# Column sums on one core: the framework's own semaphores, and a block's two rows added before the sum so far

## The chip, the cores and the metric

One core of a Trainium2 chip. The metric is device time in microseconds (us) for one execution. Every time below is a median over several executions; every run that lists a state was in the fast one, and the granted TensorE clock was 0.997 to 1.000 in every profile that the argument rests on, so clock plays no part.

## The reference

```python
x = np.random.randn(8192, 8192).astype(np.float32)
def reference(x):
    return np.sum(x, axis=0)
```

256 MiB have to be read once, and 32 KB are written. There is almost nothing to compute.

## The kernel before

The 8192 rows are cut into 32 blocks of 256 rows. A block is a tile of 128 partitions by K = 2 rows by 8192 columns (64 KB per partition, 8.39 MB). The kernel uses three such buffers. VectorE adds each block into a running sum with two adds of 128x8192; for the last block TensorE does the sum across partitions (a matmul with ones), in strips, so that little is left after the last byte arrives. Loads are issued by SyncE. Synchronisation is by hand, inside one critical section, with a loop on VectorE:

```python
def block(b):
    r0, r1 = bufs[b][:, 0, :], bufs[b][:, 1, :]
    take(s_buf[b], 17)            # this block has landed (16) and the sum so far is ready (1)
    nc.vector.tensor_tensor(out=r0, in0=r0, in1=bufs[(b - 1) % NBUF][:, 1, :], op=ADD
        ).then_inc(s_op, 1)       # first add: row 0 + the sum so far, from the previous buffer
    take(s_op, 1)
    nc.vector.sem_inc(s_free, 1)  # the previous buffer is free
    nc.vector.tensor_tensor(out=r1, in0=r1, in1=r0, op=ADD
        ).then_inc(s_buf[(b + 1) % NBUF], 1)   # second add: row 1 + that

# ... cut ...
for t in range(last):
    i = nc.sync.dma_start(out=bufs[t % NBUF][:], in_=xr[t])
    if t >= NBUF:
        i._wait_ge(s_free, t - NBUF + 1)       # a load waits until its buffer is free
    i.then_inc(s_buf[t % NBUF], 16)
# ... cut: the last block's strips, matmuls, copies and stores ...
```

## Time and profile before

| | before |
|---|---|
| time, median of 3 (lowest to highest) | 628.84 us (628.51 to 630.31) |
| span of the profiled run | 626.6 us |
| load queue's packets, share of 16 DMA engines' span | 99.1% |
| VectorE busy | 530.8 us, 85% |

The page of the profiled run, cut to four lines. The first `q1` line is the load queue: packets, megabytes, share of the 16 engines' span. An `L...` line is a group of instructions: line, engine, operation, shapes, count, then busy us and mean ns of one, then idle us just before them and what ended it. The last line is a group of loads with the median us from issue to landing.

```profile
span 626.6 us, 548 instructions
...
q1 hardware_dynamic: 6144, 268.47, 99.1%
...
L115 DVE TENSOR_TENSOR buf<-buf,buf 128x8192 f32<-128x8192 f32 x29 | 252.1, 8693 | 58.4 <-DVEq L110 58.4
L120 DVE TENSOR_TENSOR buf<-buf 128x8192 f32<-128x8192 f32 x29 | 252.1, 8693 | 6.9 <-DVEq L110 6.9
...
buf<-in_x_dram SPq DMA_DIRECT2D x31, 29.7
```

The reader should see three things. Loading is the limit: the queue's packets fill 99.1% of the engines' time. VectorE's two adds take 17.4 us of a block and it then waits about 2 us (58.4 us over 29 blocks), so it is close behind but not the limit. And a load lands 29.7 us after its issue although a block takes only 19.3: it stands in the queue for some 10 us before its turn.

VectorE's timeline (start us, duration us, what, idle before) shows the period. From one first add to the next are 119.85 to 139.16, 19.31 us:

```profile
119.85 8.69 DVE L115 TENSOR_TENSOR buf<-buf,buf 128x8192 f32<-128x8192 f32 x1 [1.66 <-DVEq L110]
128.78 8.69 DVE L120 TENSOR_TENSOR buf<-buf 128x8192 f32<-128x8192 f32 x1 [0.24 <-DVEq L110]
139.16 8.69 DVE L115 TENSOR_TENSOR buf<-buf,buf 128x8192 f32<-128x8192 f32 x1 [1.70 <-DVEq L110]
```

Three stretches by windows: up to the landing of block 2, from there to the landing of block 30 (28 blocks), and the rest. After the window's bounds come its length, the busy time of each engine, the clock, the DMA share and GB/s:

```profile
core 0: us, PE busy (x) PEld busy (x) DVE busy (x) ACT busy (x) POOL busy (x), PEclk, DMA share, GB/s
0.00:61.46 61.46, 0.00 (x0) 0.00 (x0) 26.08 (x3) 1.28 (x1) 0.33 (x5) 1.00 1.00 427
61.46:602.68 541.22, 0.00 (x0) 0.00 (x0) 486.79 (x56) 0.00 (x0) 0.00 (x0) 1.00 1.00 433
602.68:626.60 23.92, 13.58 (x136) 3.81 (x136) 17.91 (x6) 2.29 (x4) 0.00 (x0) 1.00 0.82 339
```

In the middle stretch the 16 engines are at 1.00 and move 433 GB/s; 541.22 / 28 = 19.33 us a block.

### The profile page before, as it was taken

The page shows a single profiled execution, that of the slowest core. Times are in us where ns is not written, and L with a number is a line of the kernel's source. Part 1 is how long each engine was busy: PE and PEld are TensorE (multiplying, and loading weights), DVE is VectorE, ACT ScalarE, POOL GpSimd, SP SyncE. Part 2 cuts the span into 40 slices and gives each one's busy share as a digit, 9 for nine tenths or more (in the row PEclk, how much of TensorE's full clock was granted, in tenths as well). Part 3 has the DMA queues.
Part 4 walks back from the last instruction along what each step waited for, and adds up shares of the span by engine and source line. Part 5 has one row for each costly group of instructions (what it writes and reads, how often), then busy time and mean ns, then how long its engine had stood idle before and what let it go on. Part 6 is the DMA issues. An engine that isn't in the chain of part 4 may idle for free. (4 is left out here: it accounts for less than half of the span.)

```text
span 626.6 us, 548 instructions
## 1 busy us (share of the span) xinstructions
PE 13.6 (2%) x136; PEld 3.8 (1%) x136; DVE 530.8 (85%) x65; ACT 3.6 (1%) x5; POOL 0.3 (0%) x5
## 2 busy tenths in 40 slices
PE   0000000000000000000000000000000000000026
PEld 0000000000000000000000000000000000000002
DVE  0538988889888899888898888988889988889886
ACT  0000000000000000000000000000000000000001
POOL 0000000000000000000000000000000000000000
PEclk9999999999999999999999999999999999999999
DMA  9999999999999999999999999999999999999987
GB/s 402 402 469 402 469 402 464 406 456 414 448 423 443 427 435 435 431 439 406 464 402 469 402 469 402 469 402 469 402 469 402 469 402 469 402 469 402 469 382 291
DMA packets 6153, 268.49 MB, mean 428 GB/s; under 512 B 636, under 2 KB 892, under 8 KB 1416
## 3 DMA queue, kind: packets, MB, share of 16 engines
q1 hardware_dynamic: 6144, 268.47, 99.1%
q8 instruction: 1, 0.02, 0.0%
q10 hardware_dynamic: 8, 0.00, 0.0%
HBM read 268.44 MB, written 0.03 MB: 428 GB/s over the span
## 5 line engine op out<-in xcount | busy, mean ns | idle before, releaser
L115 DVE TENSOR_TENSOR buf<-buf,buf 128x8192 f32<-128x8192 f32 x29 | 252.1, 8693 | 58.4 <-DVEq L110 58.4
L120 DVE TENSOR_TENSOR buf<-buf 128x8192 f32<-128x8192 f32 x29 | 252.1, 8693 | 6.9 <-DVEq L110 6.9
L126 DVE TENSOR_TENSOR buf<-buf 128x8192 f32<-128x8192 f32 x1 | 8.7, 8693 | 23.0 <-DVEq L110 23.0
L93 PE MATMUL ps<-buf,ones 128*32 128x512 f32 (+4 forms) x136 | 13.6, 549 | 609.4 <-DMA buf<-in_x_dram 609.0
L72 DVE TENSOR_TENSOR buf<-buf,buf 128x4096 f32<-128x4096 f32 x2 | 8.8, 4423 | 1.6 <-DMA buf<-in_x_dram 1.6
L72 DVE TENSOR_TENSOR buf<-buf 128x2048 f32<-128x2048 f32 (+1 forms) x3 | 8.9, 3001 | 0.1
L93 PEld LDWEIGHTS ps<-buf,ones 128*32 128x32 f32 x136 | 3.8, 118 | 619.0 <-DMA buf<-in_x_dram 611.7
L201 ACT COPY res<-ps 128x512 f32<-128x512 f32 (+1 forms) x4 | 2.3, 573 | 618.8 <-PE ps L93 618.8
L205 DVE COPY res<-ps 128x64 f32<-128x64 f32 x1 | 0.2, 225 | 2.6 <-PE ps L93 2.6
L201 ACT ACT_TABLE_LOAD x1 | 1.3, 1283 | 0.9 <-SPq L100 0.9
L101 POOL MEMSET ones<- 128x32 f32 x1 | 0.1, 124 | 0.5 <-SPq L100 0.5
L238 POOL MEMSET const-bfloat16-1.0<- 128x1 bf16 x1 | 0.1, 101 | 0.0
L238 POOL MEMSET const-uint8-127<- 128x1 uint8 x1 | 0.1, 101 | 0.0
L238 POOL MEMSET const-float32-0.0<- 128x1 f32 x1 | 0.1, 98 | 0.2 <-issue 0.2
L238 POOL MEMSET const-float32-1.0<- 128x1 f32 x1 | 0.1, 98 | 0.0
## 6 DMA issues: line engine op xcount, KB each, us to landing
buf<-in_x_dram SPq DMA_DIRECT2D x3, 2048.0 KB, 19.4
buf<-in_x_dram SPq DMA_DIRECT2D x1, 1024.0 KB, 25.5
buf<-in_x_dram SPq DMA_DIRECT2D x1, 768.0 KB, 26.8
buf<-in_x_dram SPq DMA_DIRECT2D x31, 29.7
buf<-in_x_dram SPq DMA_DIRECT2D x1, 256.0 KB, 22.6
out_dram<-res SPq DMA_DIRECT2D x1, 24.0 KB
out_dram<-res ACTq DMA_DIRECT2D x1, 1.0 KB
out_dram<-res SPq DMA_DIRECT2D x1, 7.0 KB
```

Source lines behind the costliest of these rows:

```text
L72: i = nc.vector.tensor_tensor(out=o, in0=a, in1=b, op=ADD)
L93: i = nc.tensor.matmul(out=o, lhsT=ones[:], rhs=r, start=start, stop=True, skip_group_check=True)
L101: nc.gpsimd.memset(ones[:], 1.0).then_inc(s_one, 1)
L115: nc.vector.tensor_tensor(out=r0, in0=r0, in1=bufs[(b - 1) % NBUF][:, 1, :], op=ADD).then_inc(s_op, 1)
L120: nc.vector.tensor_tensor(out=r1, in0=r1, in1=r0, op=ADD).then_inc(s_buf[(b + 1) % NBUF], 1)
L126: nc.vector.tensor_tensor(out=rows(0, 1), in0=rows(0, 1), in1=rows(0, 0), op=ADD).then_inc(s_buf[1], 1)
L201: i = nc.scalar.copy(res[:, 512 * g : 512 * g + w], ps[g][:, 0:w])
L205: i = nc.vector.tensor_copy(out=res[:, fin], in_=ps[4][:, 0:NI])
L238: nc = _bacc.Bacc("TRN2", target_bir_lowering=False, num_devices=1)
```

## The change

The intent is the same kernel without hand-made synchronisation: the framework (Tile) places the semaphores and frees the buffers, no critical section, no loop, the order of instructions on each engine kept by edges without semaphores. Along with this, the running sum moves from row 1 to row 0, and the two adds of a block change places: first the block's own two rows, then the sum so far. Strips and the order of the last matmuls change slightly, and two matmuls are added that only keep TensorE busy.

The diff, cut to its core:

```diff
-        def block(b):
-            r0, r1 = bufs[b][:, 0, :], bufs[b][:, 1, :]
-            take(s_buf[b], 17)
-            nc.vector.tensor_tensor(
-                out=r0, in0=r0, in1=bufs[(b - 1) % NBUF][:, 1, :], op=ADD
-            ).then_inc(s_op, 1)
-            take(s_op, 1)
-            nc.vector.sem_inc(s_free, 1)
-            nc.vector.tensor_tensor(out=r1, in0=r1, in1=r0, op=ADD).then_inc(
-                s_buf[(b + 1) % NBUF], 1
-            )
...
+    load_pool = ctx.enter_context(tc.tile_pool(name="loads", bufs=3))
...
+    prev = None
+    for t in range(T - 2):
+        xt = load_pool.tile([P, K, C], F32, tag="xt")
+        nc.sync.dma_start(out=xt, in_=xr[t])
+        add(xt[:, 0], xt[:, 0], xt[:, 1])
+        if prev is not None:
+            add(xt[:, 0], xt[:, 0], prev[:, 0])
+        prev = xt
+    near = load_pool.tile([P, K, C], F32, tag="xt")
+    nc.sync.dma_start(out=near, in_=xr[T - 2])
...
-STRIPS = [2048, 2048, 2048, 1024, 768, 256]
+STRIPS = [2048, 2048, 2048, 896, 896, 256]
...
+    keep_busy(last[:, 1, 0:512], 2)
```

The previous buffer is read by the add that takes in the sum so far. When that add comes first, the buffer is free after one add; when it comes second, after two.

More of the change, by code (lines that the diff above doesn't have):

```diff
@@ L12 @@
 K = 2
-NBUF = 3
+NJ = 4
 GROUP = 2048
-NJ = 4
-UNIT = 256
-NI = UNIT // NJ
-STRIPS = [2048, 2048, 2048, 1024, 768, 256]
+STRIPS = [2048, 2048, 2048, 896, 896, 256]
+START = [sum(STRIPS[:n]) for n in range(len(STRIPS))]
 @with_exitstack
@@ L32 @@
     T = R // (P * K)
-    near, last = T - 2, T - 1
     xr = x.rearrange("(b p k) c -> b p k c", p=P, k=K)
-    pool = ctx.enter_context(tc.tile_pool(name="sb", bufs=1))
+    const_pool = ctx.enter_context(tc.tile_pool(name="const", bufs=1))
+    load_pool = ctx.enter_context(tc.tile_pool(name="loads", bufs=3))
     psum_pool = ctx.enter_context(
@@ L41 @@
     )
-    ones = pool.tile([P, 32], F32, name="ones", tag="ones")
-    bufs = [
-        pool.tile([P, K, C], F32, name=f"buf{b}", tag=f"buf{b}") for b in range(NBUF)
-    ]
-    res = pool.tile([P, C // NJ], F32, name="res", tag="res")
-    ps = [
-        psum_pool.tile([P, 512], F32, name=f"ps{g}", tag=f"ps{g}") for g in range(5)
-    ]
-    s_buf = [nc.alloc_semaphore(f"s_buf{b}") for b in range(NBUF)]
-    s_strip = [nc.alloc_semaphore(f"s_strip{i}") for i in range(len(STRIPS))]
-    s_one = nc.alloc_semaphore("s_one")
@@ L56 @@
-    s_op = nc.alloc_semaphore("s_op")
-    s_free = nc.alloc_semaphore("s_free")
-    s_dve = nc.alloc_semaphore("s_dve")
-    s_pe = nc.alloc_semaphore("s_pe")
-    s_act = nc.alloc_semaphore("s_act")
-    s_end = nc.alloc_semaphore("s_end")
-    s_out = nc.alloc_semaphore("s_out")
-    def rows(t, k, c0=0, w=None):
-        return bufs[t % NBUF][:, k, c0 : C if w is None else c0 + w]
-    n_dve = 0
-    def vadd(o, a, b, sem, val):
-        nonlocal n_dve
-        i = nc.vector.tensor_tensor(out=o, in0=a, in1=b, op=ADD)
-        i._wait_ge(sem, val)
-        i.then_inc(s_dve, 1)
-        n_dve += 1
-        return n_dve
@@ L78, in column_sums @@
-    def column_sums(src, c0, w, start, sem=None, val=0):
-        g, f = divmod(c0, GROUP)
-        for j in range(NJ):
-            if g < 3:
-                assert (f, w) == (0, GROUP)
-                o = ps[g][32 * j : 32 * j + 32, :]
-                r = src[:, c0 + 512 * j : c0 + 512 * j + 512]
-            else:
-                u, n = f // UNIT, w // UNIT
-                b, q = (4, 0) if u == 7 else (3, u)
-                o = ps[b][32 * j : 32 * j + 32, NI * q : NI * (q + n)]
-                r = src[:, c0 : c0 + w].rearrange("p (u j i) -> p j u i", j=NJ, i=NI)[
-                    :, j
-                ]
-            i = nc.tensor.matmul(
-                out=o, lhsT=ones[:], rhs=r, start=start, stop=True, skip_group_check=True
-            )
-            if sem is not None and j == 0:
-                i._wait_ge(sem, val)
-        return i
@@ L100 @@
-    with tc.tile_critical():
-        nc.gpsimd.memset(ones[:], 1.0).then_inc(s_one, 1)
-        def take(sem, n):
-            nc.vector.sem_inc(sem, -n)._wait_ge(sem, n)
-        def block(b):
-            r0, r1 = bufs[b][:, 0, :], bufs[b][:, 1, :]
-            take(s_buf[b], 17)
-            nc.vector.tensor_tensor(
-                out=r0, in0=r0, in1=bufs[(b - 1) % NBUF][:, 1, :], op=ADD
-            ).then_inc(s_op, 1)
-            take(s_op, 1)
-            nc.vector.sem_inc(s_free, 1)
-            nc.vector.tensor_tensor(out=r1, in0=r1, in1=r0, op=ADD).then_inc(
-                s_buf[(b + 1) % NBUF], 1
-            )
-        assert near % NBUF == 0
-        take(s_buf[0], 16)
-        nc.vector.tensor_tensor(
-            out=rows(0, 1), in0=rows(0, 1), in1=rows(0, 0), op=ADD
-        ).then_inc(s_buf[1], 1)
-        for b in range(1, NBUF):
-            block(b)
-        with nc.vector.Fori(0, near // NBUF - 1):
-            for b in range(NBUF):
-                block(b)
-        carry = {}
-        for c0, parts in ((0, ((0, 2 * GROUP),)), (2 * GROUP, ((3, GROUP), (2, GROUP)))):
-            w = 2 * GROUP
-            d = vadd(
-                rows(near, 0, c0, w),
-                rows(near, 0, c0, w),
-                rows(near - 1, 1, c0, w),
-                s_buf[near % NBUF],
-                17,
-            )
-            for g, gw in parts:
-                v = vadd(
-                    rows(near, 1, g * GROUP, gw),
-                    rows(near, 1, g * GROUP, gw),
-                    rows(near, 0, g * GROUP, gw),
-                    s_dve,
-                    d,
-                )
-                for i in range(gw // GROUP):
-                    carry[g + i] = v
-        for t in range(last):
-            i = nc.sync.dma_start(out=bufs[t % NBUF][:], in_=xr[t])
-            if t >= NBUF:
-                i._wait_ge(s_free, t - NBUF + 1)
-            i.then_inc(s_buf[t % NBUF], 16)
-        c0 = 0
-        for n, w in enumerate(STRIPS):
-            i = nc.sync.dma_start(
-                out=bufs[last % NBUF][:, :, c0 : c0 + w], in_=xr[last][:, :, c0 : c0 + w]
-            )
-            if n == 0:
-                i._wait_ge(s_free, last - NBUF + 1)
-            i.then_inc(s_strip[n], 16)
-            c0 += w
-        def strip_sums(n, start):
-            c0 = sum(STRIPS[:n])
-            column_sums(rows(last, 0), c0, STRIPS[n], start, s_strip[n], 16)
-            return column_sums(rows(last, 1), c0, STRIPS[n], False)
-        def carry_sums(g, start):
-            if g < 3:
-                return column_sums(
-                    rows(near, 1), g * GROUP, GROUP, start, s_dve, carry[g]
-                )
-            column_sums(rows(near, 1), 3 * GROUP, 7 * UNIT, start, s_dve, carry[g])
-            return column_sums(rows(near, 1), 3 * GROUP + 7 * UNIT, UNIT, start)
-        nc.tensor.wait_ge(s_one, 1)
-        strip_sums(0, True)
-        carry_sums(0, False).then_inc(s_pe, 1)
-        strip_sums(1, True)
-        carry_sums(1, False).then_inc(s_pe, 1)
-        strip_sums(2, True)
-        carry_sums(3, True)
-        strip_sums(3, False)
-        carry_sums(2, False).then_inc(s_pe, 1)
-        strip_sums(4, False).then_inc(s_pe, 1)
-        strip_sums(5, False).then_inc(s_pe, 1)
-        for n, (g, w) in enumerate(((0, 512), (1, 512), (2, 512), (3, 7 * NI))):
-            i = nc.scalar.copy(res[:, 512 * g : 512 * g + w], ps[g][:, 0:w])
-            i._wait_ge(s_pe, n + 1)
-            i.then_inc(s_act, 1)
-        fin = slice(512 * 3 + 7 * NI, 512 * 4)
-        i = nc.vector.tensor_copy(out=res[:, fin], in_=ps[4][:, 0:NI])
-        i._wait_ge(s_pe, 5)
-        i.then_inc(s_end, 1)
-        lanes = slice(0, 32 * (NJ - 1) + 1, 32)
-        nc.sync.dma_start(
-            out=out[0 : 3 * GROUP].rearrange("(g j i) -> j g i", g=3, j=NJ),
-            in_=res[lanes, 0 : 3 * 512].rearrange("j (g i) -> j g i", g=3),
-        )._wait_ge(s_act, 3).then_inc(s_out, 16)
-        nc.sync.dma_start(
-            out=out[3 * GROUP : C - UNIT].rearrange("(u j i) -> j u i", j=NJ, i=NI),
-            in_=res[lanes, 3 * 512 : 3 * 512 + 7 * NI].rearrange(
-                "j (u i) -> j u i", i=NI
-            ),
-        )._wait_ge(s_act, 4).then_inc(s_out, 16)
-        nc.scalar.dma_start(
-            out=out[C - UNIT :].rearrange("(j i) -> j i", j=NJ), in_=res[lanes, fin]
-        )._wait_ge(s_end, 1).then_inc(s_out, 16)
-        nc.sync.wait_ge(s_out, 48)
@@ new lines, with in_order @@
+    ones = const_pool.tile([P, 32], F32)
+    nc.gpsimd.memset(ones, 1.0)
+    ps = [
+        psum_pool.tile([P, 512], F32, name=f"ps{n}", tag=f"ps{n}")
+        for n in range(len(STRIPS) + 1)
+    ]
+    res = [
+        const_pool.tile([P, w], F32, name=f"res{n}", tag=f"res{n}")
+        for n, w in enumerate((3 * 512, 2 * STRIPS[3] // NJ, STRIPS[5] // NJ))
+    ]
+    newest = {}
+    def in_order(engine, i):
+        if engine in newest:
+            tc.add_manual_dep(
+                i.ins,
+                newest[engine].name,
+                mybir.DependencyInfo(
+                    mybir.DependencyClass.NoSync, mybir.DependencyReason.SCHED_ONLY
+                ),
+            )
+        newest[engine] = i.ins
@@ new lines, in add, with piece_sums @@
+    def add(o, a, b):
+        in_order("DVE", nc.vector.tensor_tensor(out=o, in0=a, in1=b, op=ADD))
+    def piece_sums(src, n, start, stop=False):
+        w = STRIPS[n] // NJ
+        for j in range(NJ):
+            i = nc.tensor.matmul(
+                out=ps[n][32 * j : 32 * j + 32, 0:w],
+                lhsT=ones,
+                rhs=src[:, START[n] + j * w : START[n] + (j + 1) * w],
+                start=start,
+                stop=stop,
+                skip_group_check=True,
+            )
+            in_order("PE", i)
@@ new lines, in keep_busy @@
+    def keep_busy(src, turns):
+        for _ in range(turns):
+            i = nc.tensor.matmul(
+                out=ps[len(STRIPS)][0:32, :],
+                lhsT=ones,
+                rhs=src,
+                start=True,
+                stop=True,
+            )
+            in_order("PE", i)
+    prev = None
[6 more added lines that the diff above has]
+        prev = xt
@@ new lines, with fold, carry_in @@
+    near = load_pool.tile([P, K, C], F32, tag="xt")
+    nc.sync.dma_start(out=near, in_=xr[T - 2])
+    last = load_pool.tile([P, K, C], F32, tag="xt")
+    for c0, w in zip(START, STRIPS):
+        nc.sync.dma_start(
+            out=last[:, :, c0 : c0 + w], in_=xr[T - 1][:, :, c0 : c0 + w]
+        )
+    def fold(c0, w):
+        add(near[:, 0, c0 : c0 + w], near[:, 0, c0 : c0 + w], near[:, 1, c0 : c0 + w])
+    def carry_in(c0, w):
+        add(near[:, 0, c0 : c0 + w], near[:, 0, c0 : c0 + w], prev[:, 0, c0 : c0 + w])
@@ new lines, in strip_sums, with evacuate, store @@
+    def strip_sums(n, stop=False):
+        piece_sums(last[:, 0], n, False)
+        piece_sums(last[:, 1], n, False, stop)
+    def evacuate(copy, n, r, f):
+        w = STRIPS[n] // NJ
+        copy(out=res[r][:, f : f + w], in_=ps[n][:, 0:w])
+    def store(eng, n, count, r):
+        w = STRIPS[n] // NJ
+        eng.dma_start(
+            out=out[START[n] : START[n] + count * STRIPS[n]].rearrange(
+                "(g j i) -> j g i", j=NJ, i=w
+            ),
+            in_=res[r][0 : 32 * (NJ - 1) + 1 : 32, :].rearrange(
+                "j (g i) -> j g i", i=w
+            ),
+        )
@@ new lines @@
+    fold(0, 2 * GROUP)
+    carry_in(0, 2 * GROUP)
+    fold(2 * GROUP, 2 * GROUP)
+    carry_in(3 * GROUP, GROUP)
+    carry_in(2 * GROUP, GROUP)
+    for n in (0, 1):
+        piece_sums(last[:, 0], n, True)
+        piece_sums(last[:, 1], n, False)
+        piece_sums(near[:, 0], n, False, True)
+        evacuate(nc.scalar.copy, n, 0, 512 * n)
+    keep_busy(last[:, 1, 0:512], 2)
+    piece_sums(last[:, 0], 2, True)
+    piece_sums(last[:, 1], 2, False)
+    for n in (3, 4, 5):
+        piece_sums(near[:, 0], n, True)
@@ L227 @@
+    strip_sums(3, True)
+    evacuate(nc.scalar.copy, 3, 1, 0)
+    piece_sums(near[:, 0], 2, False, True)
+    evacuate(nc.scalar.copy, 2, 0, 1024)
+    store(nc.sync, 0, 3, 0)
+    strip_sums(4, True)
+    evacuate(nc.scalar.copy, 4, 1, STRIPS[3] // NJ)
+    store(nc.sync, 3, 2, 1)
+    strip_sums(5, True)
+    evacuate(nc.vector.tensor_copy, 5, 2, 0)
+    store(nc.scalar, 5, 1, 2)
 _INS = ['x']
```

## The prediction

> **What bounds the kernel now.** Loading x. The page shows 268.47 MB on the load queue, its packets taking 99.1% of the 16 DMA engines' span; VectorE is 85% busy, PE 2%. In the packet records a 65,536-byte packet takes 2.418 us, so 16 engines move 433.6 GB/s. (The Trainium skill, "DMA: Bandwidth & Descriptors", Specifications, gives a fabric ceiling of 435 GB/s; the trace agrees.) A block is 8 packets per engine, 19.34 us; landings are 19.32 us apart. 32 blocks are 619 of the span's 626.6 us. The time can hardly fall; it rises if the engines run dry.
>
> **What the change does to that.** In a block (timeline of VectorE) the first add starts 0.14 us after the landing L, each add takes 8.69 us, 0.24 us lies between the two. Today the *first* add reads the previous sum, so that buffer is freed after one add: SyncE issues the next load at L + 9.0. The next block lands at L + 19.3, so the load waits in the queue and no engine sees a gap.
> After the change the *second* add reads it. Waits sit on the adds themselves, as today in the block before last (start 0.02 us after landing, about 0.03 us between dependent adds), so 0.3 us per block goes. The buffer comes free at L + 17.43, issue at L + 17.5: 8.5 us later. VectorE, 17.4 us of 19.3, stays off the critical path.
>
> **Is L + 17.5 early enough?** Not quite. (Same page, Anatomy of one DMA: waits happen on the issuing sequencer, engines only consume their queues.) In this trace the first load's packets start 0.6 us after its issue instruction (0.33 us in later loads) ends, so here at L + 18.45 to 18.65. Engines write the last packet of the block in flight at L + 18.5 to 19.0 (landings spread 0.45 us and come 0.35 us after the packet's end). First packets on idle engines took 2.97 to 3.36 us instead of 2.418, so about 0.6 us of start latency is hidden only if descriptors arrive that far ahead; they arrive 0.1 to 0.3 us ahead. The very first load took 21.86 us from issue to landing; with two loads alternating, a period is at most (17.5 + 21.86)/2 = 19.68 us. I estimate a bubble of 0.2 us per block (0 to 0.35), times 28 or 29: +6 us (0 to +10). The last block's first strip, issued as late (0.6 us per issue): +0.3 us.
>
> **Rest.** No critical section: its entry costs SyncE about 0.2 us before the first issue, its exit and second barrier some 0.4 us: -0.6 us. The unrolled loop, two PE matmuls that keep it busy, the new strips and split results run behind the last loads: 0 +/- 0.3 us.
>
> **Prediction.** 634 us (before 628.84), 8 times in 10 between 629 and 639. Chances: faster by over 2% 0.01, within 2% 0.93, slower by over 2% 0.06.
>
> **What would show it.** Right: issue-to-landing of the loads falls from 29.7 to about 21.5 us; landings 19.4 to 19.7 us apart; packets start with gaps, or each block's first packets take over 2.418 us; load share below 99%; VectorE gaps of 0.03 and about 2 us. Wrong: landings still 19.32 us apart (then about 628.3), or 20 us and more.
>
> **What would make it wrong.** A start behind a nearly empty queue that is faster or slower than the first one; a costlier wait between dependent adds (0.1 us would cost 0.05 us per block); two waits on one issue; a longer tail.

## The result, and the profile after

| | before | after |
|---|---|---|
| time, median of 6 (lowest to highest) | 628.81 us (628.51 to 630.31) | 667.67 us (664.68 to 671.04) |
| ratio, 95% interval | | 1.0611 (1.0571 to 1.0651) |
| span of the profiled run | 626.6 us | 664.3 us |
| load queue's packets, share of engines' span | 99.1% | 95.8% |
| VectorE busy | 530.8 us | 530.7 us |

A ratio here and below is the mean time of one kernel's fast runs over the mean of the other's in the same rounds, so it is not quite the ratio of the medians quoted beside it.

The change costs 39 us, 6%, at the same amount of VectorE work. The same lines of the page:

```profile
span 664.3 us, 488 instructions
...
q1 hardware_dynamic: 6124, 268.47, 95.8%
...
L66 DVE TENSOR_TENSOR xt<-xt 128x8192 f32<-128x8192 f32 x59 | 512.8, 8692 | 122.2 <-DMA xt<-in_x_dram 121.2
...
xt<-in_x_dram SPq DMA_DIRECT2D x30, 24.3
```

Loads now take 24.3 us from issue to landing instead of 29.7, so they no longer stand in the queue, but it is also more than the 21.9 us that the very first load of either kernel needed on idle engines. VectorE waits 121.2 us for loads. Before it was 58.4 + 23.0 = 81.4 us (the page puts these waits on VectorE's own queue, because the hand-made waits are instructions there), plus 6.9 us between dependent adds.

The same windows show where it happened, in the middle stretch: 578.37 us instead of 541.22, 20.66 us a block, at 0.96 of the engines and 406 GB/s. The first stretch gained 0.2 us and the last lost 0.75.

```profile
core 0: us, PE busy (x) PEld busy (x) DVE busy (x) ACT busy (x) POOL busy (x), PEclk, DMA share, GB/s
0.00:61.26 61.26, 0.00 (x0) 0.00 (x0) 26.07 (x3) 1.28 (x1) 0.33 (x5) 1.00 0.99 423
61.26:639.63 578.37, 0.00 (x0) 0.00 (x0) 486.75 (x56) 0.00 (x0) 0.00 (x0) 1.00 0.96 406
639.63:664.30 24.67, 15.14 (x148) 4.70 (x148) 17.90 (x6) 2.45 (x5) 0.00 (x0) 0.97 0.78 309
```

The chain that ended last looks different too: before, it went back through the last loads only (DMA 4% of the span, then it met a wait of SyncE); now it alternates through the whole run between loads and adds:

```profile
DMA 59%; DVE 39%; SPq 1%; issue 0%; PE 0%
DMA xt<-in_x_dram 56%; DVE xt L66 39%; DMA last<-in_x_dram 3%; SPq L109 0%; PE ps L72 0%; SPq L100 0%; DVE res L125 0%
```

This difference must not be taken for the cause. tile_two_tiles, below, shows the same chain (DMA 56%, DVE 42%) and is as fast as the kernel before; raw_free_late, which is as slow as the changed kernel, shows the short one (DMA 3%). The chain breaks off early where the waits are made by hand, whatever the time.

VectorE's timeline (two adds merged into one line of 17.42 us) shows that the loss is not even. Some blocks come 19.4 us after the one before, others 22.6 us after:

```profile
103.00 17.42 DVE L66 TENSOR_TENSOR xt<-xt 128x8192 f32<-128x8192 f32 x2 [2.37 <-DMA xt<-in_x_dram]
122.39 17.42 DVE L66 TENSOR_TENSOR xt<-xt 128x8192 f32<-128x8192 f32 x2 [1.97 <-DMA xt<-in_x_dram]
144.98 17.42 DVE L66 TENSOR_TENSOR xt<-xt 128x8192 f32<-128x8192 f32 x2 [5.17 <-DMA xt<-in_x_dram]
164.93 17.42 DVE L66 TENSOR_TENSOR xt<-xt 128x8192 f32<-128x8192 f32 x2 [2.52 <-DMA xt<-in_x_dram]
```

To see why, one has to look at the single increments of a load's semaphore in the trace. The Trainium skill ("DMA: Bandwidth & Descriptors", "Why a DMA increments its semaphore by 16 and not by 1") says that each of the 16 engines adds one when its own share of the load has landed; the trace agrees in that each load has 16 separate increments. Worked out from those records, in us (L is the landing of the block two before, that is of the block whose adds free the buffer):

```
kernel  load  issue-L  issue   1st    8th    15th   16th landing   issue to 16th
before   12     9.00   225.31  254.52 254.59 254.85 254.99         29.68
after     5    17.47   100.66  121.78 122.10 122.36 122.37         21.72
after     6    17.47   120.45  141.78 141.96 142.18 144.96         24.51
after     7    17.47   139.84  161.10 161.38 161.79 164.90         25.06
after     8    17.47   162.43  183.49 183.92 184.18 184.22         21.80
```

In load 6, fifteen engines land within 0.4 us and one lands 2.8 us later. The block is complete only when that one is in, so its adds, the release and the issue of load 8 (162.43) wait for it; the other fifteen engines have landed load 7 by 161.79 and run dry. In the packet records this late engine begins its share 3.45 us after the issue (123.90), where the others begin at 0.98 to 1.64. I call this a late engine, and count a load as having one when its 16 landings spread over more than 1.2 us: 21 of the 28 loads of the middle stretch in the changed kernel, none of 28 before.

The count needs care: a late share is not always a late start. Load 7 is late as well, but between loads 6 and 7 no engine paused (by the packet records, idle time summed over the 16 engines is under 0.1 us); its late share began late because the same share of load 6 was still being moved. The same holds for 9 of the 21 loads (at most 0.11 us of idle time, summed); they were issued 4.0 to 5.7 us before the load in flight landed. In the other 12 the engines did pause, 1.9 us or more in sum. So a late start in one load is often seen twice.

### The profile page after: what moved, and what is told of

Read it like the earlier page. It is cut to its first block, busy times and chain, and to the rows that moved or that the text cites. A ratio compares the mean times of both kernels' runs of the same rounds, so it can differ in the third digit from the quotient of the medians.

```text
span 664.3 us, 488 instructions
## 1 busy us (share of the span) xinstructions
PE 15.1 (2%) x148; PEld 4.7 (1%) x148; DVE 530.7 (80%) x65; ACT 3.7 (1%) x6; POOL 0.3 (0%) x5
## 3 DMA queue, kind: packets, MB, share of 16 engines
q1 hardware_dynamic: 6124, 268.47, 95.8%
## 4 chain that ended last, share of the span: by engine, by line
DMA 59%; DVE 39%; SPq 1%; issue 0%; PE 0%
DMA xt<-in_x_dram 56%; DVE xt L66 39%; DMA last<-in_x_dram 3%; SPq L109 0%; PE ps L72 0%; SPq L100 0%; DVE res L125 0%
## 5 line engine op out<-in xcount | busy, mean ns | idle before, releaser
L66 DVE TENSOR_TENSOR xt<-xt 128x8192 f32<-128x8192 f32 x59 | 512.8, 8692 | 122.2 <-DMA xt<-in_x_dram 121.2
L72 PE MATMUL ps<-last,ones 128*32 128x512 f32 (+2 forms) x96 | 9.6, 531 | 645.8 <-DMA last<-in_x_dram 645.8
L66 DVE TENSOR_TENSOR near<-near 128x4096 f32<-128x4096 f32 x2 | 8.8, 4421 | 4.6 <-DMA near<-in_x_dram 4.6
L66 DVE TENSOR_TENSOR near<-near,xt 128x2048 f32<-128x2048 f32 (+1 forms) x3 | 8.9, 3000 | 0.1
L72 PEld LDWEIGHTS ps<-last,ones 128*32 128x32 f32 x96 | 2.8, 117 | 651.5 <-issue 647.3
L72 PE MATMUL ps<-near,ones 128*32 128x512 f32 (+2 forms) x48 | 4.5, 482 | 0.2 <-DVE near L66 0.2
L85 PE MATMUL ps<-last,ones 128*32 128x512 f32 x4 | 1.9, 592 | 0.0
L72 PEld LDWEIGHTS ps<-near,ones 128*32 128x32 f32 x48 | 1.5, 115 | 3.5 <-DVE near L66 1.9
L85 PEld LDWEIGHTS ps<-last,ones 128*32 128x32 f32 x4 | 0.4, 110 | 1.3 <-issue 1.3
## 6 DMA issues: line engine op xcount, KB each, us to landing
xt<-in_x_dram SPq DMA_DIRECT2D x30, 24.3
```

The source lines that it names most:

```text
L66: in_order("DVE", nc.vector.tensor_tensor(out=o, in0=a, in1=b, op=ADD))
L72: i = nc.tensor.matmul(out=ps[n][32 * j : 32 * j + 32, 0:w], lhsT=ones, rhs=src[:, START[n] + j * w : START[n] + (j + 1) * w], start=start ...
L85: i = nc.tensor.matmul(out=ps[len(STRIPS)][0:32, :], lhsT=ones, rhs=src, start=True, stop=True,)
```

## The experiments

An accounting that holds for all of them: load t is issued a time d after the landing of block t-2 (it waits for that block's adds) and lands a time I after its issue, so two periods are d + I and one is (d + I)/2. The accounting counts times; it does not say why I is what it is. For the changed kernel, with d = 17.47 and a mean I of 23.75: 20.61 us, against 20.66 measured. The question is always what d is and what I becomes.

The theories:
- **A**: the late release of the buffer is the whole loss. **B**: the framework's own semaphores, waits and unrolled stream cost it. **C**: what the adds read and write costs it, not when the buffer is freed.
- **D**: late engines arise because a load is put into the very queue that is just running empty. **S**: late engines arise only when a load arrives shortly before the engines run dry; on engines that are idle already, or well fed, there are none. **P**: that window is the last packet (2.4 us). **W**: it is a time, whatever the packet.

### Is it the release? (four runs)

**tile_sum_first**, the changed kernel with the two adds put back in the old order:

```diff
-        add(xt[:, 0], xt[:, 0], xt[:, 1])
         if prev is not None:
             add(xt[:, 0], xt[:, 0], prev[:, 0])
+        add(xt[:, 0], xt[:, 0], xt[:, 1])
```

> The changed kernel with only the order of a block's two adds put back (sum so far first). Theory A (the late release of the buffer is the whole loss): loads are issued about 8.8 us after a landing again, landings 19.32 us apart, 628 us (0.5 us less than before for the missing section). Rival B (Tile's own semaphores, two waits per load issue, unrolled stream): stays at 655 to 670 us. Part each: in between.

Measured: 628.83 us, before 628.3 us, ratio 1.0006 (0.9989 to 1.0022). Its page, same lines as above:

```profile
q1 hardware_dynamic: 6124, 268.47, 99.1%
...
xt<-in_x_dram SPq DMA_DIRECT2D x30, 29.8
```

The share is back at 99.1% and the loads stand in the queue again (29.8 us). Two lines exchanged give back all 39 us. B falls: no cost of Tile's semaphores shows (the interval leaves room for about a microsecond). The half microsecond that I expected to gain from the missing section did not show either.

**raw_rows_first**, the kernel before with nothing but the new order (calls shortened in the diffs of the raw kernels, here and below):

```diff
-            tensor_tensor(out=r0, in0=r0, in1=previous r1).then_inc(s_op, 1)
-            take(s_op, 1)
-            sem_inc(s_free, 1)
-            tensor_tensor(out=r1, in0=r1, in1=r0).then_inc(s_buf[next], 1)
+            tensor_tensor(out=r0, in0=r0, in1=r1).then_inc(s_op, 1)
+            take(s_op, 1)
+            tensor_tensor(out=r1, in0=r0, in1=previous r1).then_inc(s_op, 1)
+            take(s_op, 1)
+            sem_inc(s_free, 1)
+            sem_inc(s_buf[next], 1)
```

> The kernel before (own semaphores, section, loop) with only the order of the adds changed: rows first, sum so far second, buffer released after the second. Release at 18.0 us after the landing. Theory A: 660 to 675 us, issue to landing 21.7 to 25 us. Rival B: 629 to 632 us.

Measured: 671.97 us, ratio 1.0678 (1.0646 to 1.0709).

**raw_free_late**, the kernel before with its old order, only the release signalled later:

```diff
             tensor_tensor(out=r0, in0=r0, in1=previous r1).then_inc(s_op, 1)
             take(s_op, 1)
-            sem_inc(s_free, 1)
-            tensor_tensor(out=r1, in0=r1, in1=r0).then_inc(s_buf[next], 1)
+            tensor_tensor(out=r1, in0=r1, in1=r0).then_inc(s_op, 1)
+            take(s_op, 1)
+            sem_inc(s_free, 1)
+            sem_inc(s_buf[next], 1)
```

> The kernel before with its order of adds, but the release of the buffer signalled after the second add instead of the first; the data order is as before. Theory A: same time as raw_rows_first within 5 us (660 to 675). If it is what the adds read and write that matters (rival C), 629 to 632 us.

Measured: 672.71 us, ratio 1.071 (1.0692 to 1.0728). The same as raw_rows_first, with the data flow of the fast kernel. So C falls too, and A stands from both sides: taking the late release out of the changed kernel gives everything back, putting it alone into the kernel before costs everything. (These two release at 17.84 us, 0.4 later than the changed kernel, because the hand-made waits lie between their adds.)

**tile_two_queues**, the changed kernel with odd loads from t = 3 on issued by ScalarE:

```diff
-        nc.sync.dma_start(out=xt, in_=xr[t])
+        (nc.scalar if t > 2 and t % 2 else nc.sync).dma_start(out=xt, in_=xr[t])
```

> The changed kernel with odd loads from t=3 on issued by ScalarE instead of SyncE, so that a load never goes to a queue whose last load is just ending. Theory D (part of the loss, about 25 of 36 us, is that one or two engines restart up to 3 us late when their own queue ran empty just as the next load arrived): late engines vanish, landing spread 0.5 us in all blocks, time 635 to 645 us. Without D: still 660 to 670 us with spreads of 2 to 4 us in most blocks.

Measured: 674.21 us, ratio 1.0709 (1.0661 to 1.0757). The time is a clear miss for D, although loads with a late engine fell from 21 to 6 of 28. The landings show a confound: they came alternately 24.8 and 16.9 us apart, and the 24 us from issue to landing stayed. Two queues on the same engines take turns, so a load that arrives early slows the one before it. (The Trainium skill, "DMA: Bandwidth & Descriptors", "Issuing engines are not separate DMA queues", says that DMAs from different engines interleave on the same 16; the alternating landings agree.) The run says that a second queue is no cure; it doesn't settle where late engines come from.

### How late is too late? (three runs)

The kernel before, with its second add cut in two and the release signalled between the pieces, so that d can be set:

```diff
             take(s_op, 1)
-            sem_inc(s_free, 1)
-            tensor_tensor(out=r1, in0=r1, in1=r0).then_inc(s_buf[next], 1)
+            h = 6144                       # or 7168, 5120, 4096
+            tensor_tensor(out=r1[:, 0:h], in0=r1[:, 0:h], in1=r0[:, 0:h]).then_inc(s_op, 1)
+            take(s_op, 1)
+            sem_inc(s_free, 1)
+            tensor_tensor(out=r1[:, h:C], in0=r1[:, h:C], in1=r0[:, h:C]).then_inc(s_buf[next], 1)
```

**raw_free_6144**

> The kernel before with its second add cut at 6144 columns and the release signalled between the pieces: issue at about 15.9 us after the landing. Theory A with a threshold: descriptors reach the engines at 16.9, they run out at 18.5 to 19.0, so nothing is lost: 628 to 630 us. If the loss grew smoothly with the delay from 9 to 18 us, about 660 us.

Measured: 643.15 us, ratio 1.0214 (1.0183 to 1.0246), which is slower, though not clearly by more than 2%. **A miss**: I had expected no loss, because the descriptors come about 2 us before the engines run dry. 25 of 28 loads had a late engine.

**raw_free_7168**

> The same cut at 7168 columns: issue at about 17.0 us after the landing, descriptors 0.4 to 0.9 us ahead of the end of the last packets. Theory A: the edge, 629 to 642 us, packets start without a gap in most blocks, few late engines.

Measured: 654.43 us, ratio 1.0402 (1.0358 to 1.0446). **A miss** in the same direction; 24 of 28 loads with a late engine.

**raw_free_late_plus_2048**, which goes the other way: raw_free_late with a useless add ahead of the release.

```diff
             tensor_tensor(out=r1, in0=r1, in1=r0).then_inc(s_op, 1)
             take(s_op, 1)
+            tensor_tensor(out=res[:, 0:2048], in0=r1[:, 0:2048], in1=r0[:, 0:2048]).then_inc(s_op, 1)
+            take(s_op, 1)
             sem_inc(s_free, 1)
```

> raw_free_late with a useless 128x2048 add before the release: issue about 20.5 us after the landing, when the engines have already been idle. Theory S (engines restart late only when the descriptors arrive just as their last packet ends): landing spread stays at 0.5 to 0.8 us in most blocks, issue to landing 21.9 us, period (20.5 + 21.9)/2 = 21.2 us, time about 681 us, only 8 to 10 us over raw_free_late for a release 2.5 us later. Rival (late restarts come with any restart): spreads of 2 to 4 us as before, 22 us a block, about 705 us.

Measured: 680.42 us, ratio 1.0808 (1.079 to 1.0826), no load with a late engine, issue to landing 21.78 us in the median. S hit, 681 was expected. Late engines do not come with every restart: on engines that had run dry, a load's 16 landings spread over at most 1.06 us.

### A cure that keeps the order of adds

**tile_two_tiles**: the changed kernel with a block's two rows as two tiles of three buffers each, loaded by two loads, row 1 first. Row 1's buffer is free after the first add; only row 0, which carries the sum, is held through the second. (The diff is simplified; in the run a helper makes the two tiles, and the last two blocks are split in the same way.)

```diff
-        xt = load_pool.tile([P, K, C], F32, tag="xt")
-        nc.sync.dma_start(out=xt, in_=xr[t])
-        add(xt[:, 0], xt[:, 0], xt[:, 1])
+        r1 = load_pool.tile([P, C], F32, tag="row1")
+        r0 = load_pool.tile([P, C], F32, tag="row0")
+        nc.sync.dma_start(out=r1, in_=xr[t][:, 1])
+        nc.sync.dma_start(out=r0, in_=xr[t][:, 0])
+        add(r0, r0, r1)
         if prev is not None:
-            add(xt[:, 0], xt[:, 0], prev[:, 0])
+            add(r0, r0, prev)
```

> The changed kernel, same order of adds, but a block's two rows are two tiles with a load each (row 1 first), so a quarter of the buffer space is already free after the first add and a half-block load is always queued. Theory A: the engines never run dry although the sum's buffer is still freed 17.5 us after the landing: 627.5 to 630 us, landings every 9.67 us. If the order of the adds itself costs: stays at 660 or more.

Measured: 629.63 us, ratio 1.0005 (0.9986 to 1.0024). Its middle stretch, the same 28 blocks:

```profile
61.30:603.25 541.95, 0.00 (x0) 0.00 (x0) 486.74 (x56) 0.00 (x0) 0.00 (x0) 1.00 1.00 433
```

433 GB/s again, with the order of adds that cost 6% before. So the order of adds by itself costs nothing, as long as something is always queued.

### The window (four runs, then three)

**raw_free_4096**

> The cut at 4096 columns: issue at about 13.7 us after the landing. Theory P (a load costs nothing only if its descriptors reach an engine before that engine begins the last 2.4 us packet of the load in flight, that is before about 16.1 us; from the 15.9 us run, where descriptors came at 16.9 and 14 us were lost): 628 to 630.5 us. If the loss grows smoothly from 9 us on, about 638 us.

Measured: 629.0 us, ratio 1.0004 (0.9987 to 1.0021), no late engine. A hit; there is an edge, not a smooth loss.

**raw_free_late_plus_1024**, the useless add with 1024 columns:

> raw_free_late with a useless add half as long: issue about 19.3 to 19.4 us after the landing. Theory S (late engines only when the load arrives while engines are in their last packet): period (19.4 + 21.9)/2 = 20.65 us, 664 to 670 us, that is no slower than raw_free_late (672.7), though the release is 1.3 us later. If the time followed the release alone: between 672.7 and 680.4, about 676 to 677 us.

Measured: 667.12 us, ratio 1.0616 (1.0594 to 1.0639), no late engine. Faster than raw_free_late (672.71), with a release 1.4 us later and more work. S hit again.

**tile_row_loads** and **tile_half_columns**, the changed kernel with each block loaded by two loads into the same tile, so the release stays as it is and only the packets shrink (32 KB and 16 KB instead of 64):

```diff
-        nc.sync.dma_start(out=xt, in_=xr[t])
+        for k in (1, 0):
+            nc.sync.dma_start(out=xt[:, k], in_=xr[t][:, k])
```

```diff
-        nc.sync.dma_start(out=xt, in_=xr[t])
+        for c in (0, C // 2):
+            nc.sync.dma_start(out=xt[:, :, c : c + C // 2], in_=xr[t][:, :, c : c + C // 2])
```

> The changed kernel with each block loaded by two loads, one for each row (32 KB packets instead of 64 KB), both waiting for the same release 17.5 us after the landing; one tile. Theory P: lateness shrinks with the packet, engines at most 1.2 us late instead of 2.4 to 3, 640 to 655 us. If the loss is the start of a load alone, whatever the packet: 660 to 672 us, as the changed kernel. If splitting by itself were what helped tile_two_tiles: 628 to 630 us.

Measured: 664.66 us, ratio 1.0555 (1.0528 to 1.0582).

> The changed kernel with each block loaded by two loads, one for each half of the columns (16 KB packets), same release. An issue takes 0.6 us instead of 0.33, so descriptors come 0.3 us later. Theory P: engines at most 0.6 us late, period 19.5 to 19.9 us, 633 to 648 us. Else 665 us or more.

Measured: 665.37 us, ratio 1.0599 (1.0561 to 1.0638). Both speak against P, and show that splitting a load is not what cured tile_two_tiles; the earlier release of half the space is.

**raw_free_6144_rows** asks the same at the front edge: raw_free_6144 with each load split by rows.

```diff
-            i = nc.sync.dma_start(out=bufs[t % NBUF][:], in_=xr[t])
+            for k in (0, 1):
+                i = nc.sync.dma_start(out=bufs[t % NBUF][:, k], in_=xr[t][:, k])
```

> raw_free_6144 (issue 15.7 us after the landing, 643 us, 14 us lost) with each block loaded by two loads, one per row, 32 KB packets of 1.2 us instead of 2.4. The descriptors arrive about 1.8 us before the engines run dry. Theory P (window is the last packet): now they arrive before the last packet begins, 628 to 632 us. Theory W (window is a fixed time, whatever the packet): 640 to 647 us, landing spreads of about 2 us as before.

Measured: 644.17 us, ratio 1.0223 (1.0165 to 1.0281), late engines in 26 of 28 blocks. P has fallen: halving the packet changes nothing. W was not refuted, which is all that can be said for it.

**raw_free_5120**

> The cut at 5120 columns: issue 14.65 us after the landing, descriptors about 2.6 to 3.2 us before the engines run dry. A window of 2.4 us, of either theory: 628 to 632 us. If the window begins earlier (between the 3.7 us of raw_free_4096 and this): 634 to 640 us.

Measured: 629.73 us, ratio 0.9995 (0.9971 to 1.0019), no late engine. So the front edge lies between d = 14.64 and 15.71 us.

**raw_free_late_plus_512**

> raw_free_late with a useless 128x512 add: issue about 18.7 us after the landing. Between raw_free_late (17.84: 672.7 us, late engines in 22 of 28 blocks) and late_plus_1024 (19.22: 667.1 us, none). If late engines thin out gradually: 662 to 671 us, late in 5 to 15 blocks. Without any late engine it would be about 655 us ((18.7 + 21.8)/2 = 20.25 us a block); with as many as raw_free_late about 680 us.

Measured: 658.42 us, ratio 1.0451 (1.0418 to 1.0483); 4 of 28 loads with a late engine. It came out below the expected range: late engines had thinned out faster than I thought. The two groups of loads, raw_free_late first, then this kernel:

```profile
buf<-in_x_dram SPq DMA_DIRECT2D x31, 23.9
```

```profile
buf<-in_x_dram SPq DMA_DIRECT2D x31, 21.9
```

A release 0.84 us *later* lets each load land 2 us sooner after its issue, and the kernel is 14 us faster.

### The same in the changed kernel itself

**tile_useless_add**

```diff
         if prev is not None:
             add(xt[:, 0], xt[:, 0], prev[:, 0])
+            add(idle, xt[:, 0, 0:1024], prev[:, 0, 0:1024])     # idle is a scratch tile
```

> The changed kernel plus a useless 128x1024 add after a block's second add that also reads the sum so far, so the release comes at 18.7 us after the landing instead of 17.5, as in raw_free_late_plus_512 (658.4 us). If late engines make part of the changed kernel's loss: 655 to 662 us, faster than the changed kernel's 667.7 with more work in it; landing spread about 0.55 us; issue to landing 21.9 us. If a later release can only cost: 675 us or more.

Measured: 660.8 us, ratio 1.0513 (1.0469 to 1.0556), against 667.67 us for the changed kernel in an earlier job. The ratios to the kernel before, 1.0513 and 1.0611, have intervals that do not overlap. Its timeline:

```profile
204.37 17.42 DVE L67 TENSOR_TENSOR xt<-xt 128x8192 f32<-128x8192 f32 x2 [2.41 <-DMA xt<-in_x_dram]
221.83 1.23 DVE L67 TENSOR_TENSOR idle<-xt 128x1024 f32<-128x1024 f32 x1
224.07 17.42 DVE L67 TENSOR_TENSOR xt<-xt 128x8192 f32<-128x8192 f32 x2 [1.02 <-DMA xt<-in_x_dram]
241.52 1.22 DVE L67 TENSOR_TENSOR idle<-xt 128x1024 f32<-128x1024 f32 x1
244.85 17.42 DVE L67 TENSOR_TENSOR xt<-xt 128x8192 f32<-128x8192 f32 x2 [2.11 <-DMA xt<-in_x_dram]
```

Each block has 1.23 us of work added, and the starts are 19.70 and 20.78 us apart, where the changed kernel had steps of 22.6. Late engines are in 3 of 28 loads instead of 21.

### All in one table

Sorted by d (the median). I is the mean from issue to landing, the period is that of the middle stretch, all from the one profiled run of each kernel; the time is the median of its runs. The jobs ran on several chips; the kernel before took 628.3 to 630.1 us in them, so differences of a microsecond or two between jobs mean nothing.

| kernel | d, us | I, us | period, us | loads with a late engine, of 28 | time, us |
|---|---|---|---|---|---|
| tile_sum_first | 8.81 | 29.89 | 19.35 | 10 | 628.8 |
| before | 9.01 | 29.65 | 19.33 | 0 | 628.8 |
| raw_free_4096 | 13.58 | 25.08 | 19.33 | 0 | 629.0 |
| raw_free_5120 | 14.64 | 24.03 | 19.34 | 0 | 629.7 |
| raw_free_6144 | 15.71 | 23.93 | 19.83 | 25 | 643.2 |
| raw_free_7168 | 16.78 | 23.49 | 20.17 | 24 | 654.4 |
| **after** | 17.47 | 23.75 | 20.66 | 21 | 667.7 |
| raw_rows_first | 17.84 | 23.68 | 20.83 | 24 | 672.0 |
| raw_free_late | 17.84 | 23.59 | 20.72 | 22 | 672.7 |
| raw_free_late_plus_512 | 18.68 | 22.00 | 20.35 | 4 | 658.4 |
| tile_useless_add | 18.73 | 22.05 | 20.42 | 3 | 660.8 |
| raw_free_late_plus_1024 | 19.22 | 21.78 | 20.51 | 0 | 667.1 |
| raw_free_late_plus_2048 | 20.28 | 21.82 | 21.10 | 0 | 680.4 |

Up to d = 14.64, I falls by as much as d grows: the load only stands in the queue for a shorter time, and nothing is lost. Between 15.71 and 17.84, I sticks at 23.5 to 23.9. From 18.7 on it is 21.8 to 22.1, the start on idle engines. The change put the kernel inside the bad window.

The count in tile_sum_first is a warning: ten of its loads pass the 1.2 us mark (none above 1.33 us) with no idle engine before any of them and no time lost. (tile_two_tiles has four such loads, at most 1.32 us.) So a spread of landings by itself need not cost anything.

Nor is a late share the same thing at both ends of the window. In raw_free_6144 the 16 engines were hardly ever idle in the middle stretch (share 0.99, against 0.96 in the changed kernel), and yet they moved only 423 GB/s:

```profile
61.46:616.77 555.31, 0.00 (x0) 0.00 (x0) 491.18 (x84) 0.00 (x0) 0.00 (x0) 1.00 0.99 423
```

Summed from the packet records, its 14.1 us over the kernel before are 3.4 us of idle engines (mean of the 16) and 10.7 us of packets that took longer: the first of a load's eight packets took 2.67 us in the mean, not 2.42. In the changed kernel the 37.1 us are 21.2 us of idle engines and 15.9 us of longer packets. So at the front edge the late shares are in the main slow first packets; idle engines weigh more only further in.

No version beat the kernel before: tile_sum_first (1.0006), tile_two_tiles (1.0005) and raw_free_5120 (0.9995) all equal it within their intervals.

## Why the prediction was wrong

- **What bounds the kernel: right.** Loading, at 433 GB/s; and no version went faster.
- **What the change moves: right.** I had the buffer free at L + 17.43 and the issue at L + 17.5; the trace has 17.47. The gap within a pair of adds was as predicted too (the pair takes 17.42 us, 0.3 us per block goes); the gap before it was not: it had been predicted at about 2 us, and in the middle stretch it was 1.85 to 5.78. That the late release alone makes the loss is shown by three runs (tile_sum_first, raw_rows_first, raw_free_late).
- **"Is L + 17.5 early enough? Not quite": right in direction, and this is where the size failed.** The step that failed is "The very first load took 21.86 us from issue to landing; with two loads alternating, a period is at most (17.5 + 21.86)/2 = 19.68 us". I took the start on idle engines for the worst case and everything earlier for something better. The term that was mis-sized is the time from issue to landing: 23.75 us in the mean, not at most 21.86. The period was 20.66 us, 1.33 us a block over before instead of "0.2 us per block (0 to 0.35)".
- **What stood in its place:** engines that finish their share of a load 1 to 3 us after the others when the load reaches them shortly before they run dry, and a block waits for its last engine. 21 of 28 loads had a late share: 12 after a pause of engines, 9 carried over from the load before. On idle engines, as in the first load that I had measured, this does not happen (0 of 28 in two runs). I had no measurement inside that window, and filled it by reasoning from its two ends.
- **The two parts of the loss, as an estimate:** with d = 17.47 and the I of 21.8 that loads had outside the window, the period would be 19.635 us, 0.305 over before, or 8.5 us in 28 blocks. That is about the +6 us of the prediction. The other 28.6 of the middle stretch's 37.15 us (578.37 - 541.22) are then put down to the late engines. This is a split by accounting. By the packet records the same 37.1 us are 21.2 us of idle engines and 15.9 us of longer packets, and no run tells how much of each a late share brings about.
- **The rest: wrong in sign, of little weight.** The first stretch was 0.2 us shorter, as predicted; the last was 0.75 us longer, where +0.3 us (first strip) and -0.4 us (exit) had been expected. tile_sum_first, with the same start and end, was not faster than before either.
- **What I named as a danger** was "a start behind a nearly empty queue that is faster or slower than the first one". It was named, and then given no room in the range.
- **Open:** why single engines start late, or take longer over a first packet, in that window. It is not the packet's size (three runs), and it is not a matter of any restart (on idle engines the landings of a load stayed within 1.06 us). The profile does not name the engines, so whether it is always the same ones stays open too. tile_two_queues could not tell whether the queue as such matters.

## What to carry to other kernels

When loading is the limit, the number to watch is not the busy share of the compute engine but how long a load stands in its queue: the time from issue to landing minus the time of the transfer itself, here some 10 us before, and next to nothing in most loads after. A reordering that leaves every engine's work as it was can still move the last read of a buffer, and with it the next load's issue; read the buffer to be freed first, or split it so that a part is freed early. And don't estimate the cost of an almost empty queue from a start on idle engines: here a release at 17.84 us cost 14 us more than one 0.84 us later.

## What the Trainium skill lacked or had wrong

- "DMA: Bandwidth & Descriptors", "Queues, rings and completion order": it lacks that a load which reaches the engines shortly before they run dry can land late on one or a few of them, after a late start or after first packets that took longer. Here, for issues 15.71 to 17.84 us after the landing two before, at 19.33 us a block, loads took 23.5 to 23.9 us from issue to landing, with landings spread over more than 1.2 us in 21 to 25 of 28 loads (in part carried over from the load before); at 18.68 and 18.73 us in 4 and 3, at 14.64 us and from 19.22 us on in none.
- The same page, "Rules for kernel authors": overlap is advised in general ("Issue the DMA early"), and it lacks how early. Here, with 8.39 MB loads, an issue 4.7 us before the landing of the load in flight (19.33 - 14.64) lost nothing, and one 3.6 us before it (19.33 - 15.71), which is what a load after an undelayed one gets, lost 2%.
- The same page, "Anatomy of one DMA — SWDGE (gpsimd) path": its fit of 2.0 us + bytes / 436e3 gives 21.2 us for 8.39 MB (an estimate from that page, for the other issue path). A fit for loads issued by SyncE is lacking; on idle engines they took 21.8 us.

Two figures were compared and agree. "DMA: Bandwidth & Descriptors", Specifications: the fabric ceiling of 435 GB/s agrees; the middle stretch of the fast kernels moved 433 GB/s. "VectorE: DVE Perf Modes", "The perf-mode tier table (the rule you actually need)": 2293 ns for an fp32 add of 2048 columns agrees; the useless add of 128x2048 took 2292 ns.
